# Last four gates and six query blocks as five Strassen pairs ahead of the state-space scan

## The chip, the cores and the metric

The kernel runs on one core of one Trainium2 chip. The metric is the device time of one execution in microseconds. PE is TensorE (its weight loads are shown as PEld), DVE is VectorE, ACT is ScalarE, POOL is GpSimd and SP is SyncE, which here mostly issues DMAs. "Us" counts from the start of the profiled span.

## The reference

One layer of a decoder for a prompt of 1024 tokens and a sample group of 8 tokens, 1032 columns in all, model width 1024, all in float32:

```python
sc_b, sc_c, sc_x, z, xbc, dt_raw, q, gates = jnp.split(xn @ w_in, splits, axis=-1)
y_a = (sc_b * conv_u) @ w_sc_out                       # gated convolution
y_ssd, ssm_new = ssd_fn(xs, dt, a, bm, cm, ssm_s0)     # chunked scan, 32 heads in 4 groups, 8 chunks of 128
y_ssd = (y_ssd + ssm_d[:, None] * xs).reshape(...) * jax.nn.silu(z)
y_b = group_rmsnorm(y_ssd, ssm_norm_w, SSM_GROUPS) @ w_ssm_out
y_c = jnp.einsum('bhlm,bmhd->blhd', probs, mem_v).reshape(...) @ w_attn_o
g_a, g_b, g_c = jnp.split(jax.nn.sigmoid(gates), N_BRANCHES, axis=-1)
merged = g_a * y_a + g_b * y_b + g_c * y_c             # then w_merge_o, the SwiGLU block, the last norm
```

The change concerns the columns `q` (1024, eight blocks of 128) and `gates` (3072, 24 blocks of 128) of the first product, and how the scan `ssd_fn` shares the time with products.

## The kernel before, in words

Activations lie transposed: 128 features on the partitions, 1032 columns. Every product is made with three passes (high by high, low by high, high by low parts of a float32 split in two), so a weight block is first split by one ACT cast (L167) and one DVE subtraction (L168).

A **plain block** (`gemm`, L199, matmuls of L219) makes 128 output features: 8 slices of the contraction by 3 passes by 3 column pieces (256, 512, 264), which is 72 matmuls into one of two PSUM buffers (`pmm`, L64). A **Strassen pair** (`strassen`, L310, matmuls of L265) makes two such blocks at once with 7 half-size products instead of 8: 7 by 4 slices by 3 passes by 2 pieces (256, 260), 168 matmuls, and some more additions on DVE and ACT. Nearly all blocks of the first product run as pairs, the last one being `gate_pair(18)`, tile names G18. Its hook `plain` (L1371) turns the activations back into the plain form and loads the data of the scan's first group.

Then comes the **scan stage**. Its products are 12 plain `fillers` (L1387: the eight query blocks, tiles `ps_q`, weights wq0 to wq7, and the gate blocks 20 to 23, tiles `ps_g`) and after them the `outs`: the eight blocks of the convolution's output product (weights wo00 to wo07), eight and eight of the state-space output product's two halves (wo10 to wo17 and wo20 to wo27), and the eight of the attention output (wo30 to wo37). The scan itself is cut into small pieces in the queue `pend`, 158 in all. While a plain block is recorded, `tick` (L183) takes pieces out of that queue; `pace` (L1470) sets how many for each block: `len(pend) / (len(fillers) + KD)`, KD being 8, so 158 pieces over 20 blocks. The later attention stage does the same with its own pieces (L1697): all of them over the blocks of `outs` that are still left, less one.

A chunk of the scan has three pieces. `first` (L996): PE makes bp (a transpose and the C by B product) and xp (four transposes); DVE makes cbm (L1008), multiplies it onto the decays r (L1011) and makes xdt (L1013); POOL makes xdd. `third` (L1049) of the chunk before: PE makes pss, DVE adds it to the state s (L1059). `second` (L1022): PE makes po from the state and py from r and xdt, DVE puts both into y (L1036, L1045). The decays are loaded (L979, 512 KB broadcast) and prepared on ACT (L985, L986).

Between two groups of heads lies a **turn**: `z_pieces` (L1126) and `group_norm` (L1146) on the finished group (DVE products and sums into sqa, then PE psny, a root on ACT, PE psnr, ACT copies, the DVE scaling L1177 and four stores to `yb_d`), and the load of the next group's data (L1364, L1368) into tiles that the finished group has held. The next group's chunk 0 needs them.

The inputs of the output products are read back from DRAM tile by tile ahead of time: `out_ahead` (L1411) loads two tiles, and hangs a function on the next block that splits tile k-2 and loads tile k while slice k is recorded (L1416). These tiles, called in00 to in07, like most evictions, come from the pool `ev` of five buffers (L60), which also holds the sums sqa and the final state sf of each group. The tiles b00 to b07 are their split forms and the moving operands of the blocks. The two halves of the state-space product read `yb_d`, which groups 1 and 2 and then groups 3 and 4 of the scan have written.

All of this is recorded as one program, and a scheduler then places the instructions engine by engine: what is recorded first goes first if it can, otherwise later work goes ahead. The resulting order on each engine and in each DMA queue is fixed in the built program.

## Time and profile before

| | |
|---|---|
| Time, median of 3 runs | 2478.05 us (2475.4 to 2478.8) |
| The profiled execution | 2481.63 us, its span 2479.3 us |
| PE busy in the span | 98% |
| DVE, ACT, POOL busy | 64%, 43%, 5% |
| DMA, mean over the span | 163 GB/s |
| G18, the last pair, starts | 940.0 us |
| wq0, first plain block of the scan stage, starts | 960.8 us |
| wo10, first block of the state-space output, starts | 1317.4 us |
| wo30, first block of the attention output, starts | 1586.3 us |

PE is busy nearly everywhere, so the program is read as PE's own work plus the short times in which PE waits. A row of the timeline gives start, duration, engine, line, operation, out<-in by the program's names, and in brackets how long the engine was idle before it and for whom.

### The profile page before, as it was taken

What the parts mean: (1) busy time and instruction counts of PE and PEld (TensorE: products, weight loads), DVE (VectorE), ACT (ScalarE), POOL (GpSimd) and SP (SyncE); (2) the same over time, 40 slices, a digit from 0 to 9 for tenths busy, and PEclk for the clock granted to TensorE, in tenths of its full rate; (3) what the DMA queues carried; (4) which work ended last, traced back from release to release, by engine and by line L of the source; (5) the groups of instructions that cost most, each with busy time, mean ns of one, the idle gap of its engine ahead of it and who ended that gap; (6) DMA issues with size and microseconds to landing.
All of it is one profiled execution on the core that took longest, in us unless ns stands there. A gap on an engine that the chain in (4) does not pass through costs nothing.

```text
span 2479.3 us, 45686 instructions
## 1 busy us (share of the span) xinstructions
PE 2433.7 (98%) x18946; PEld 2312.4 (93%) x18946; DVE 1586.1 (64%) x2601; ACT 1067.9 (43%) x1714; POOL 114.3 (5%) x163
## 2 busy tenths in 40 slices
PE   8999999999999999999999999999999999999998
PEld 6899999999999999888888887899999999999998
DVE  6744586777677774667767562454787555476755
ACT  6554455453555535556445441223443333342322
POOL 0100000000000000121120000000000000000000
PEclk9999999999999999999999999999999999999999
DMA  6344435344344456668878687774453323264421
GB/s 197 112 145 154 129 103 154 111 128 117 123 132 142 128 154 209 194 207 267 264 217 275 204 272 238 258 239 154 143 174 129 112 82 112 77 234 127 154 85 69
DMA packets 359662, 404.42 MB, mean 163 GB/s; under 512 B 17446, under 2 KB 286870, under 8 KB 359447
## 3 DMA queue, kind: packets, MB, share of 16 engines
q1 hardware_dynamic: 339006, 343.79, 44.5%
q10 hardware_dynamic: 20449, 57.71, 6.0%
q8 instruction: 149, 2.44, 0.4%
q14 instruction: 58, 0.48, 0.1%
HBM read 286.35 MB, written 115.32 MB: 162 GB/s over the span
## 4 chain that ended last, share of the span: by engine, by line
PE 84%; DMA 6%; DVE 6%; ACT 2%; issue 1%; SPq 0%; ACTq 0%; DVEq 0%; POOL 0%
PE po L219 12%; PE ps_q L219 4%; PE pm L1799 4%; PE ps_g L219 2%; PE pd L219 1%; PE py L1040 1%; PE pss L1053 1%; PE po L1032 1%; PE Z2m L265 1%; PE d02m L265 1%; PE ps_z L219 1%; PE Z4m L265 1%; PE X8m L265 1%; PE C1m L265 1%; PE G18m L265 1%
## 5 line engine op out<-in xcount | busy, mean ns | idle before, releaser
L985 ACT ACTIVATE r<-r,acum 128x128 f32<-128x128 f32 x256 | 79.3, 392 | 4.3 <-DMA r<-ac_d 3.9
L756 DVE SCALAR_TENSOR_TENSOR ax<-u,prm,ax 128x1024 f32<-128x1024 f32 x44 | 56.4, 1281 | 0.0
L926 ACT ACTIVATE st<-st,es 128x128 f32<-128x128 f32 x128 | 41.5, 392 | 28.6 <-DMA st<-in_state_ssm_dram 23.0
L1017 POOL TENSOR_TENSOR xdd<-xdt,decst 128x512 f32<-128x512 f32 x32 | 38.9, 1215 | 287.7 <-DVE xdt L1013 287.7
L1446 DVE TENSOR_TENSOR yr<-po,yr 128x1032 f32<-128x1032 f32 x8 | 9.8, 1230 | 55.9 <-PE po L219 45.0
L1036 DVE TENSOR_TENSOR y<-po,ea 128x512 f32<-128x512 f32 x28 | 19.3, 690 | 37.5 <-PE po L1032 37.3
L1011 DVE TENSOR_TENSOR r<-r,cbm 128x1024 f32<-128x1024 f32 x32 | 39.2, 1224 | 2.4
L928 DVE SCALAR_TENSOR_TENSOR st<-sr,dts,st 128x128 f32<-128x128 f32 x128 | 40.2, 345 | 0.4
L1010 ACT COPY bT<-bp 128x128 f32<-128x128 f32 x32 | 8.5, 265 | 69.8 <-DVE cbm L1008 69.7
L2033 ACT ACTIVATE fj<-psy 128x512 f32<-128x512 f32 (+1 forms) x18 | 10.7, 595 | 59.1 <-PE psy L2031 59.0
L932 DVE SCALAR_TENSOR_TENSOR sr<-st,sr 128x128 f32<-128x128 f32 x128 | 35.3, 285 | 1.1
L1040 PE MATMUL py<-r,xdt 128*64 128x128 f32 x512 | 35.0, 279 | 0.0
L986 ACT ACTIVATE r<-r 128x1024 f32<-128x1024 f32 x32 | 33.9, 1058 | 0.6
L1053 PE MATMUL pss<-xdd,bT 128*128 128x512 f32 x64 | 33.4, 604 | 0.5 <-ACT bT L1010 0.5
L1806 DVE TENSOR_TENSOR x<-pm,xT 128x516 f32<-128x516 f32 x16 | 11.1, 695 | 35.1 <-PE pm L1799 35.1
L1013 DVE TENSOR_TENSOR xdt<-xp,dtT 128x512 f32<-128x512 f32 x32 | 21.9, 685 | 17.8 <-PE xp L1006 17.6
L1040 PEld LDWEIGHTS py<-r,xdt 128*64 128x64 f32 x512 | 27.3, 136 | 4.2 <-issue 0.5
L1032 PE MATMUL po<-bc,s 128*128 128x128 f32 x224 | 29.8, 276 | 1.0 <-DVE s L1059 1.0
L1066 POOL TENSOR_TENSOR s<-s,cdec 128x512 f32<-128x512 f32 x28 | 30.2, 1078 | 7.6 <-DVE s L1059 7.2
L1032 PEld LDWEIGHTS po<-bc,s 128*128 128x128 f32 x224 | 27.6, 191 | 2.8 <-issue 1.6
L1728 DVE TENSOR_TENSOR gt<-po,gt 128x1032 f32<-128x1032 f32 x8 | 9.8, 1231 | 30.1 <-PE po L219 27.1
L759 DVE SCALAR_TENSOR_TENSOR ax<-u,prm,ax 128x1032 f32<-128x1032 f32 x22 | 28.3, 1288 | 0.0
(9066 smaller groups left out, 8985.7 us busy)
## 6 DMA issues: line engine op xcount, KB each, us to landing
r<-ac_d SPq DMA_DIRECT2D x32, 512.0 KB
gt<-gt_d SPq DMA_DIRECT2D x24, 516.0 KB
xs_d<-ax ACTq DMA_DIRECT2D x22, 516.0 KB
gt_d<-G ACTq DMA_DIRECT2D x20, 516.0 KB
x<-xs_d SPq DMA_DIRECT2D x16, 516.0 KB
zs<-zs_d SPq DMA_DIRECT2D x16, 516.0 KB
yb_d<-x SPq DMA_DIRECT2D x16, 516.0 KB
in<-yb_d SPq DMA_DIRECT2D x16, 516.0 KB
```

Source lines behind the costliest of these rows:

```text
L219: PE.matmul(out[:, c : c + n], wt[:, ks], x[:, c : c + n], start=(k == 0 and i == 0), stop=(k == nk - 1 and i == 2),)
L265: PE.matmul(hv(ps)[:, c : c + n], wt[:, ks], x[:, c : c + n], start=(start and kt == 0 and i == 0), stop=(kt == 3 and i == 2), skip_group_ ...
L756: V.scalar_tensor_tensor(acc[:, :T], u[:, j : j + T], w[j], acc[:, :T], op0=ALU.mult, op1=ALU.add)
L926: S.activation(st[:, i], st[:, i], AF.Copy, scale=es[:, g * 4 + i, b : b + 1])
L928: V.scalar_tensor_tensor(st[:, i], rb, dts[:, g * 4 + i, b : b + 1], st[:, i], op0=ALU.mult, op1=ALU.add)
L985: S.activation(r[:, j, :], r[:, j, :], AF.Relu, scale=-1.0, bias=acum[:, c, h : h + 1])
L1011: V.tensor_tensor(r, r, bc(cbm.unsqueeze(1), [P, HPG, P]), op=ALU.mult)
L1017: G.tensor_tensor(b3(xdd, HPG), b3(xdt, HPG), bc(decst[:, c, hs].unsqueeze(2), [P, HPG, 64]), op=ALU.mult)
L1032: PE.matmul(po[:, t * P : (t + 1) * P], state["s"][:, t * P : (t + 1) * P], bcg[1][:, cs], start=True, stop=True,)
L1040: PE.matmul(py[hp : hp + 64, (h // 2) * P : (h // 2 + 1) * P], xdt[:, h * 64 : (h + 1) * 64], r[:, (h % 2) * 4 + h // 2, :], start=True, s ...
L1053: PE.matmul(pss, bT, xdd, start=True, stop=True)
L1799: PE.matmul(hv(ps)[:, c : c + n], wt[:, ks], x[:, half * HT + c : half * HT + c + n], start=(k == 0 and i == 0), stop=(k == KD - 1 and i = ...
```

## The change

Query blocks 0 to 5 and gates 20 to 23 leave the fillers and become five Strassen pairs (`q_pair`, new, and the known `gate_pair`) right after `gate_pair(16)` and ahead of `gate_pair(18)`. Two fillers stay, wq6 and wq7. The pieces of the scan are now spread over 2 + 8 + 3 = 13 blocks, three of them from the state-space output product, and the attention stage, which starts with what is left of `outs`, has its pieces spread over three blocks fewer.

```diff
--- before.py
+++ after.py
@@ -808,15 +808,6 @@
 
         return [Step(wblock(w_in, C_Q + i * P), f"wq{i}", s)]
 
-    def gate_step(i):
-        def s():
-            ps = proj(C_G + i * P, f"g{i}")
-            t = ev_tile(f"g{i}")
-            S.activation(t[:, :TT], flat(ps), AF.Sigmoid)
-            S.dma_start(gt_d[i], t[:, :TT])
-
-        return [Step(wblock(w_in, C_G + i * P), f"wg{i}", s)]
-
     def xbc_conv(ct, u, name):
         G.memset(u[:, 0:3], 0.0)
         G.tensor_copy(tail_xc[:, ct // 8, :, ct % 8], u[:, T : T + 11])
@@ -877,6 +868,21 @@
 
     def z_pair(i, hook=None):
         plain_pair(C_Z, zs_d, i, "Z", AF.Silu, hook)
+
+    def q_pair(i):
+        os = []
+
+        def outs():
+            os.extend([pa_["u"](f"Q{i}"), pa_["u"](f"Q{i + 1}")])
+            return os[0][:, HS[0]], os[0][:, HS[1]], None, os[1][:, HS[1]]
+
+        pa = strassen(
+            wblock(w_in, C_Q + i * P), wblock(w_in, C_Q + (i + 1) * P), xforms, f"Q{i}", pa_["s"], outs
+        )
+        S.activation(os[1][:, HS[0]], pa, AF.Copy, scale=-1.0)
+        for j, t in enumerate(os):
+            G.tensor_copy(qs[:, i + j, :], t[:, T:TT])
+            S.dma_start(q_d[i + j], t[:, :TT])
 
     def gate_pair(i, after_t3=None):
         plain_pair(C_G, gt_d, i, "G", AF.Sigmoid, None, after_t3)
@@ -1351,6 +1357,10 @@
     with_steps(3, lambda: z_pair(14))
     with_steps(2, lambda: gate_pair(16))
     assert not steps
+    for i in range(0, 6, 2):
+        q_pair(i)
+    for i in (20, 22):
+        gate_pair(i)
     rb = ev_tile("rb")
     SY.dma_start(rb[:, :TT], r_d.to_broadcast([P, TT]))
     b12s = []
@@ -1369,7 +1379,7 @@
             xg.append(t)
 
     def plain():
-        loaded["wq0"] = load_raw(wblock(w_in, C_Q), "wq0")
+        loaded["wq6"] = load_raw(wblock(w_in, C_Q + 6 * P), "wq6")
         load_group(0)
         for kt in range(4):
             split_to(*xforms["T3"][kt], b12s[kt // 2][:, HS[kt % 2]])
@@ -1385,10 +1395,8 @@
     for name in ("ssr", "ssd", "ssy"):
         pool[name] = ssd.enter_context(tc.tile_pool(name=name, bufs=2, side="right"))
     fillers = deque()
-    for i in range(8):
+    for i in range(6, 8):
         fillers.extend(q_step(i))
-    for i in range(20, 24):
-        fillers.extend(gate_step(i))
 
     acts = []
 
@@ -1467,7 +1475,7 @@
         pend.append(lambda g=g, hold=hold: [z_load(g, t, hold) for t in range(2)])
         pend.extend(pieces[-3:])
         pend.extend(z_pieces(g, xg, hold) + [None] + group_norm(g, xg, hold))
-    pace[:] = len(pend) / (len(fillers) + KD) + 1e-6, 0.0
+    pace[:] = len(pend) / (len(fillers) + KD + 3) + 1e-6, 0.0
     while fillers or pend:
         if len(fillers) == 1:
             out_ahead(sc_d)
```

What the scheduler makes of it, in numbers of plain matmuls that stand on PE between one py and the next (72 are one block):

| PE, scan stage | before | after |
|---|---|---|
| bp of group 1 chunk 0 to its py | 72 | 52 |
| group 2, chunks 1 to 7 | 11 13 13 22 27 27 36 | 12 13 19 13 13 13 13 |
| group 3, chunks 1 to 7 | 18 24 27 30 18 19 21 | 11 12 6 19 11 0 0 |
| turn from group 1 to 2, py to py | 202 | 214 |
| turn from group 2 to 3 | 203 | 191 |
| turn from group 3 to 4 | 220 | 71 |

The first place is PE at the end of group 3's scan (names with 2_6 and 2_7 are its chunks 6 and 7; po01 and po10 are plain blocks). Before:

```order
L1002 MATMUL bp2_7_13514<-ident_75,bc162_12830 128x128
L1003 MATMUL bp2_7_13514<-bc202_12832,bc162_12830 128x128
L219 MATMUL po01_13461<-b02h_13094,wo01l_13458 128x256
L219 MATMUL po01_13461<-b02h_13094,wo01l_13458 128x512
L219 MATMUL po01_13461<-b02h_13094,wo01l_13458 128x264
L219 MATMUL po01_13461<-b03h_13123,wo01h_13457 128x256
L1006 MATMUL xp2_7_13517<-ident_75,x20_12834 128x128
L1006 MATMUL xp2_7_13517<-ident_75,x21_12836 128x128
L1006 MATMUL xp2_7_13517<-ident_75,x22_12838 128x128
L1006 MATMUL xp2_7_13517<-ident_75,x23_12840 128x128
L219 MATMUL po01_13461<-b03h_13123,wo01h_13457 128x512
L1053 MATMUL pss2_6_13540<-xdd2_6_13441,bT2_6_13436 128x512
```

After:

```order
L1008 MATMUL bp2_7_14171<-ident_75,bc162_13627 128x128
L1009 MATMUL bp2_7_14171<-bc202_13629,bc162_13627 128x128
L1012 MATMUL xp2_7_14174<-ident_75,x20_13631 128x128
L1012 MATMUL xp2_7_14174<-ident_75,x21_13633 128x128
L1012 MATMUL xp2_7_14174<-ident_75,x22_13635 128x128
L1012 MATMUL xp2_7_14174<-ident_75,x23_13637 128x128
L1059 MATMUL pss2_6_14197<-xdd2_6_14118,bT2_6_14113 128x512
L1038 MATMUL po2_7_14215<-bc202_13629,s2_6_14132 128x128 x4
L1046 MATMUL py2_7_14221<-r2_7_14049,xdt2_7_14184 64x128 x8
L1059 MATMUL pss2_7_14240<-xdd2_7_14186,bT2_7_14181 128x512
L1081 MATMUL psf2_14266<-ident_75,s2_7_14200 128x128 x4
L219 MATMUL po10_14471<-b02h_14344,wo10h_14467 128x256
```

Before, plain matmuls of wo01 stand between the scan's. After, nothing stands between them from chunk 6 on, and the first plain matmul behind the last chunk needs b02, the split of in02.

The second place is the DMA queue of SP where the inputs of wo10 are loaded from `yb_d` (in00 to in07; r and ea are the scan's decays, 2_7 being group 3's last chunk and 3_0 to 3_2 group 4's first). Before:

```order
L1399 DMA in00_14540<-yb_d_122 128x1032
L1440 DMA mg_d_125<-gt06_14376 128x1032
L1399 DMA in01_14542<-yb_d_122 128x1032
L1533 DMA kc00_14862<-in_cache_mem_k_dram 128x1024
L1399 DMA in02_14582<-yb_d_122 128x1032
L1399 DMA in03_14601<-yb_d_122 128x1032
L1399 DMA in04_14616<-yb_d_122 128x1032
L1533 DMA kc01_14914<-in_cache_mem_k_dram 128x1024
L139 DMA wo14r_15231<-in_w_ssm_out_dram 128x8x128
L1440 DMA mg_d_125<-gt07_14538 128x1032
L1399 DMA in05_14648<-yb_d_122 128x1032
L1399 DMA in06_14663<-yb_d_122 128x1032
```

After, where in00 and in01 stand some twenty rows further up:

```order
L985 DMA r3_2_14502<-ac_d_138 128x1024
L999 DMA ea3_1_14543<-ea_d_139 64x512
L1407 DMA in02_14310<-yb_d_122 128x1032
L1084 DMA out_p_ssm_dram<-sf2_14271 128x4x128
L1407 DMA in03_14333<-yb_d_122 128x1032
L1407 DMA in04_14348<-yb_d_122 128x1032
L1374 DMA bc163_14420<-xs_d_128 128x1032
L1378 DMA x30_14424<-xs_d_128 128x1032
L1378 DMA x32_14428<-xs_d_128 128x1032
L1407 DMA in05_14380<-yb_d_122 128x1032
```

Before, the whole scan is over when these inputs are loaded. After, in02 stands behind decay loads of group 4 (chunks 1 and 2), which go into buffers that group 3's last chunks hold, and in03 and in04 behind the store of group 3's final state.

The third place is PE at the end of the attention stage, where psob transposes the sample's attention rows (they are then stored to `at_d`, from which wo30 reads). Before:

```order
L219 MATMUL po27_17129<-b01h_16033,wo27h_17125 128x256
L219 MATMUL po27_17129<-b01h_16033,wo27h_17125 128x512
L219 MATMUL po27_17129<-b01h_16033,wo27h_17125 128x264
L1607 MATMUL psob_17080<-ident_75,osr_17078 128x8 x8
L219 MATMUL po27_17129<-b01l_16034,wo27h_17125 128x256
L219 MATMUL po27_17129<-b01l_16034,wo27h_17125 128x512
L219 MATMUL po27_17129<-b01l_16034,wo27h_17125 128x264
```

After:

```order
L219 MATMUL po27_17353<-b05l_16225,wo27h_17349 128x256
L219 MATMUL po27_17353<-b05l_16225,wo27h_17349 128x512
L1615 MATMUL psob_17304<-ident_75,osr_17302 128x8 x8
L219 MATMUL po27_17353<-b05l_16225,wo27h_17349 128x264
L219 MATMUL po27_17353<-b05h_16224,wo27l_17350 128x256
L219 MATMUL po27_17353<-b05h_16224,wo27l_17350 128x512
```

Before, psob stands 12 matmuls into wo27, with 60 left; after, 50 matmuls into it, with 22 left.

## Prediction

> **What bounds the kernel now.** I read the page first, then the busy times of chosen stretches, then what PE waited for. The page's head and its first section:
>
> ```profile
> span 2479.3 us, 45686 instructions
> PE 2433.7 (98%) x18946; PEld 2312.4 (93%) x18946; DVE 1586.1 (64%) x2601; ACT 1067.9 (43%) x1714; POOL 114.3 (5%) x163
> ```
>
> PE is the bound over the whole program. So there are two sums: what PE no longer has to do, and how long it newly stands still. The stretches (from:to, length, busy time of PE, PEld, DVE, ACT and POOL with instructions, PE clock, DMA):
>
> ```profile
> 900.00:960.00 60.00, 60.00 (x507) 60.00 (x506) 32.96 (x53) 27.04 (x35) 0.00 (x0) 1.00 0.58 185
> 960.00:1317.00 357.00, 355.48 (x2561) 306.54 (x2560) 239.19 (x296) 199.54 (x413) 70.67 (x68) 1.00 0.73 231
> 1317.00:1586.00 269.00, 257.92 (x1703) 222.38 (x1702) 132.61 (x315) 95.23 (x187) 0.00 (x0) 0.99 0.74 246
> 1586.10:1589.50 3.40, 3.21 (x10) 2.51 (x11) 3.27 (x3) 2.20 (x3) 0.00 (x0) 0.50 0.39 112
> 1622.20:1667.40 45.20, 45.20 (x289) 40.99 (x288) 22.30 (x19) 6.37 (x7) 0.00 (x0) 1.00 0.70 228
> ```
>
> The first row holds three pairs of 168 matmuls: 20.0 us a pair. The last holds four plain blocks of 72: 11.3 us a block, 0.157 us a matmul. The second is the scan stage: 20 blocks are 226 us of its 357, the other 131 are the scan's own PE work, and PE stands still for 1.5 us. In the attention stage, third row, it stands still for 11. The fourth row is for the clock, below.
>
> That the scan costs PE no waiting today does not mean that it is fast. Its own rhythm is seen where it has run closest together, in group 2. All DVE instructions of one chunk there:
>
> ```profile
> 1074.75 0.69 DVE L1045 TENSOR_TENSOR y<-py,y 128x512 f32<-128x512 f32 x1 [0.34 <-PE py L1040]
> 1075.36 0.28 DVE L1008 TENSOR_TENSOR cbm<-bp,tri 128x128 f32<-128x128 f32 x1
> 1075.74 1.23 DVE L1011 TENSOR_TENSOR r<-r,cbm 128x1024 f32<-128x1024 f32 x1
> 1076.88 0.68 DVE L1013 TENSOR_TENSOR xdt<-xp,dtT 128x512 f32<-128x512 f32 x1
> 1077.49 0.68 DVE L1059 TENSOR_TENSOR s<-pss,s 128x512 f32<-128x512 f32 x1
> 1079.52 0.69 DVE L1036 TENSOR_TENSOR y<-po,ea 128x512 f32<-128x512 f32 x1 [1.36 <-PE po L1032]
> ```
>
> The next y<-py starts 1.04 us after the last row (0.69 of work, 0.34 of waiting for py, as in the first row), at 1080.56: a circle of 5.8 us. PE's po waits for s, DVE's y for po, the next cbm for y. Nothing in the circle is spare, so 5.8 us is what a chunk takes by itself. The order has 13 plain matmuls in that chunk (2.0 us), so PE's own part of a chunk is 3.8 us.
>
> The turn between two groups is slower. Chosen rows of the turn from group 1 to 2, py to py:
>
> ```profile
> 1029.76 1.09 PE L1040 MATMUL py<-r,xdt 128*64 128x128 f32 x16
> ...
> 1046.70 2.07 PE L1153 MATMUL psny<-ones,sqa 128*128 128x1 f32 x18
> ...
> 1053.98 4.91 DVE L1177 SCALAR_TENSOR_TENSOR x<-x,prm,sqa 128x1032 f32<-128x1032 f32 x4 [3.13 <-ACT sqa L1173]
> 1055.30 3.94 SPq L1180 DMA_DIRECT2D yb_d<-x  x4
> ...
> 1059.33 1.46 SPq L1368 DMA_DIRECT2D x<-xs_d  x2
> ...
> 1067.91 1.09 PE L1040 MATMUL py<-r,xdt 128*64 128x128 f32 x16
> ```
>
> The finished group is normed (17 us to psny, 7 more to the scaling, 5 of scaling), stored, and only then come the last two loads of the next group's x, into the tiles that the stores free: 38.2 us. PE does 202 plain matmuls in it, 31.7 us, and 6.5 us of the scan's.
>
> **The change part by part.**
>
> *Ten blocks become five pairs.* 10 x 11.3 = 113.0 us of PE work becomes 5 x 20.0 = 100.0: -13.0 us, and this is all that the change can gain. The pairs' additions, casts and stores cost nothing, since DVE and ACT are busy for 33 and 27 us of 60 in the first row above and DMA for 0.58 of the time; without that cover a pair would take its DVE time, 11 us, which is below 20. Their ten weight loads stand on SP's queue and their ten stores on ACT's ahead of those of G18, where before they stood among the scan's loads; nobody waits there. The scan's own instructions stay the same in number.
>
> *The start of the scan.* Before, 72 plain matmuls stand between xp and py of the first chunk, after, 52, which is 8.2 us:
>
> ```profile
> 960.84 0.74 PE L219 MATMUL ps_q<-xnh,wq0h 128*128 128x256 f32 x3
> ...
> 970.20 0.18 DVE L1083 COPY y<-ys 128x32 f32<-128x32 f32 x1 [8.55 <-DMA gt_d<-G]
> 970.30 1.22 DVE L1011 TENSOR_TENSOR r<-r,cbm 128x1024 f32<-128x1024 f32 x1
> ```
>
> DVE is stopped there until the gate tile of G18 is stored, and that is in the change as well: py can start at 971.6 at the earliest, PE would be there at 969.0. +2.6 us (0 if the store lands early, 4 if late).
>
> *Chunks of group 3.* 13 plain matmuls fill a chunk's 5.8 us. After, chunks 3 to 7 have 6, 19, 11, 0 and 0. Chunk 3 has three splits more on DVE (wo12, b00, b01; a split of a block is 1.22 us in the turn's stretch), one of them between s and po, so I give it 7.0 us: 3.8 + 0.9 of work, 2.3 us of waiting. Chunk 4 none, chunk 5 0.3, chunks 6 and 7 2.0 each. Together 6.6; I take +6 (3 if po and py answer faster in an empty queue, 9 if the splits cost in full).
>
> *The turn from group 3 to 4.* The cover of the turn is gone. The two blocks wo10 and wo11 hold both PSUM buffers, and beyond their first two slices they need in02 to in07, whose loads stand behind group 4's decays and the final state on SP. These wait for py and psf of group 3's last chunk; behind them on the same queue wait in03 to in07 and the x tiles of group 4. In the order 71 plain matmuls are left in the turn, 11.1 us, with 6.5 of the scan's: 17.6 us of work. I take the turn at 37 us: the chain above less about 1 us in which psnr had only waited its place on PE. That is 19.4 us of waiting: +19.5. Bounds: 34 us (16.5) if the last x loads land sooner, 41 us (23.5) by the slowest turn:
>
> ```profile
> 1209.59 0.66 PE L1040 MATMUL py<-r,xdt 128*64 128x128 f32 x8
> ...
> 1250.67 0.44 PE L1040 MATMUL py<-r,xdt 128*64 128x128 f32 x4
> ```
>
> *The other turns* have 214 and 191 matmuls, 33.6 and 30.0 us, with 6.5: 40 and 36.5 against 37. +1 (0 to 4).
>
> *The attention stage* has the same pieces over 12 blocks, not 15. What PE waited for there:
>
> ```profile
> PE psp L1646 <- DVE pTl L1654: 3.0, 2, 2.2
> PE psa L1632 <- ACT pr L1552: 2.8, 2, 1.7
> PE po L219 <- ACT b00h L177: 2.2, 1, 2.2
> PE pskT L1519 <- DVE kTl L1522: 1.7, 1, 1.7
> ```
>
> Without the third row this is 7.5 us of waiting for DVE and ACT. A fifth less filler between the steps makes it half as much again at a guess: +3 (0 if the pieces still fit, 8 if it doubles). DVE is busy for half of this stage, so it does not become the bound.
>
> *The end of the attention stage.* The third row is the wait of wo30 for the sample rows, whose chain begins with psob:
>
> ```profile
> 1573.76 0.66 PE L1607 MATMUL psob<-ident,osr 8*128 8x8 f32 x8
> ...
> 1578.70 3.95 SPq L1399 DMA_DIRECT2D in<-at_d  x3
> ...
> 1586.25 0.58 PE L219 MATMUL po<-b00h,wo30h 128*128 128x256 f32 x1 [2.19 <-ACT b00h L177]
> ```
>
> 12.5 us from psob to wo30, in which 60 plain matmuls (9.4 us) and psob leave 2.2 to wait. After, 22 are left: 38 fewer are 6.0 us: +6 (4 to 7).
>
> *The clock.* Right behind that wait of 2.2 us lies the row 1586.1:1589.5 with a clock of 0.50. Half the clock for 3.4 us costs at most 1.7 us where PE is busy. The turn's waiting will come in some four pieces, but PE's work there is late anyway, so only psny, psnr and xp on the chain count: +2 (0 to 6).
>
> The Trainium skill, TensorE: Matmul & The Clock Gate, Part 1, says that the clock is halved after at least one idle window of about 3.4 us. The trace halves it after 2.2 us of idleness, so here the measurement decides. By the page the short waits would keep the full clock and the sum would be 1 to 2 us lower.
>
> The sum: -13.0 + 2.6 + 6 + 19.5 + 1 + 3 + 6 + 2 = +27.1 us. The profiled execution took 2481.63 us, so 2508.7; the median is 3.6 us lower, 2478.05, and against it I forecast 2505.2.
>
> **The rivals.**
>
> *The scan answers faster than its rows (not slower).* PE was never idle in this stage, so 5.8 and 38 us may be times in PE's queue more than the scan's own. If an empty queue brought the turn down to 20 us, the waits of the turn, chunks, start and end would shrink to some 2.4, 1, 0 and 3, with 2 for attention: -13 + 8.4 = -4.6, 2473.5. It decides from a turn of about 24 us down. Against it: DVE alone is busy for most of the first 17 us and for the 5 of scaling, and the loads follow the stores.
>
> *Only the turn is shorter*, 31 us, and the clock and attention cost nothing: -13 + 2.6 + 6 + 13.5 + 6 = +15, 2493. The x loads take up to 7 us each with DMA at 0.73 of its time; with PE and its evictions still, they may take less.
>
> *The attention stage starves too.* Its steps wait on DVE, which has 133 us to do in what would be 13 x 11.3 + 77 = 224 us (257.9 less 16 blocks is 77), and the loads of the same bytes are pressed together. If its 11 us of waiting become 25, that is 11 more than my 3: +38, 2516.
>
> *The change does not do what it says*, the pairs stalling without side work: the pairs of the first row run at 20.0 us with little beside them, so this is worth 1 or 2 us at most.
>
> **How the numbers follow.** A measurement of this kernel tells 0.2%, 5 us, from no change. Forecast (2498 to 2512): 0.6. Only the turn shorter (2483 to 2498): 0.13. Attention starved (2512 to 2525): 0.17. Within 5 us: 0.05. Faster: 0.05. The range of 8 in 10 reaches from 2490 to 2519: 0.14 is left out below (faster, within 5 us and a third of the shorter turn) and 0.06 above (a third of the starved attention). Faster 0.05, same 0.05, slower 0.90.
>
> **What would show it.** Right: five pairs of 20 us each behind G16; in group 3's last two chunks a py every 5.8 us with no ps or po of a plain block between them; then a turn of some 37 us in which PE is busy for half, its waits put down to b02 to b06 and to sqa; psob less than 4 us ahead of wo27's end and 8 us of waiting for b00 behind it; clock marks of 0.50 in the turn. Wrong: a turn below 25 us, or PE idle for less than 13 us more than before. If PE waits for as long as I say, but in the attention heads, the mechanism is wrong and the size an accident.

## The result, and the profile after

| | before | after |
|---|---|---|
| Median | 2478.43 us (2475.40 to 2481.28, 4 runs) | 2518.47 us (2511.70 to 2523.83, 4 runs) |
| Profiled execution, its span | 2481.63, 2479.3 us | 2518.46, 2516.7 us |

After to before is 1.0161, 95% interval 1.0149 to 1.0173: slower by 40 us. The forecast was 2505.2 (2490 to 2519), 27.1 us slower.

The page of the kernel after, its head and first section:

```profile
span 2516.7 us, 46021 instructions
PE 2438.1 (97%) x19066; PEld 2323.1 (92%) x19066; DVE 1617.3 (64%) x2646; ACT 1074.9 (43%) x1732; POOL 117.5 (5%) x163
```

PE has 120 matmuls more (840 for five pairs less 720 for ten blocks), which should be 13 us less of work. It is busy for 4.4 us *more*. It stands still for 78.6 us instead of 45.6. Both have to be explained. Plain matmuls below are those of plain blocks (L219). Stretches of the kernel after (from:to, length, busy time of PE, PEld, DVE, ACT, POOL, then PE clock and DMA), in this order: six pairs (the five new ones and G18), the scan to the last psnr of group 4, in it the turns from group 2 to 3 and from group 3 to 4, then the attention stage to psob, and psob to wo30:

```profile
937.00:1057.00 120.00, 120.00 (x1010) 120.00 (x1010) 55.68 (x70) 42.98 (x59) 3.95 (x6) 1.00 0.43 138
1057.75:1401.10 343.35, 312.30 (x2168) 261.51 (x2167) 240.64 (x302) 187.75 (x403) 69.53 (x62) 0.94 0.73 233
1203.80:1247.90 44.10, 41.89 (x250) 36.93 (x249) 29.55 (x33) 14.26 (x23) 0.08 (x1) 0.88 0.78 257
...
1293.40:1332.20 38.80, 25.52 (x130) 20.79 (x129) 28.61 (x32) 17.15 (x26) 0.45 (x1) 0.69 0.72 253
1401.10:1615.10 214.00, 203.34 (x1340) 174.50 (x1338) 114.92 (x295) 78.34 (x169) 0.00 (x0) 0.98 0.76 255
1615.10:1625.80 10.70, 4.27 (x31) 3.66 (x30) 4.43 (x6) 1.66 (x2) 0.00 (x0) 0.85 0.90 292
```

The same two stages before (the scan to psnr of group 4, and attention to psob):

```profile
960.84:1327.90 367.06, 365.54 (x2628) 315.72 (x2627) 246.35 (x305) 204.60 (x419) 70.67 (x68) 1.00 0.74 233
1327.90:1573.80 245.90, 236.76 (x1559) 203.44 (x1559) 121.97 (x301) 87.66 (x178) 0.00 (x0) 0.99 0.72 241
```

The scan stage holds 1487 plain matmuls before and 1025 after, counted in the traces between the starts of the py groups; at 0.157 us that is 72.5 us less. The stage became only 23.7 us shorter. The other 48.8 us are the cost: PE stands still for 31.1 us in it instead of 1.5, which is 29.5, and the other 19.3 are slower work. What each part takes beyond its plain matmuls (length less 0.157 each):

| us beyond plain work | before | after | more | forecast |
|---|---|---|---|---|
| start to the first py | 0.2 | 1.4 | 1.2 | 2.6 |
| group 1, chunks 1 to 7 | 26.3 | 31.7 | 5.4 | 0 |
| turn 1 to 2 | 6.4 | 6.7 | 0.3 | together 1 |
| group 2 | 26.5 | 26.8 | 0.3 | 0 |
| turn 2 to 3 | 6.6 | 14.1 | 7.5 | (above) |
| group 3 | 28.7 | 36.2 | 7.5 | 6 |
| turn 3 to 4 | 6.5 | 27.6 | 21.1 | 19.5 |
| group 4 | 26.7 | 29.3 | 2.6 | 0 |
| last turn, to psnr | 5.6 | 8.5 | 2.9 | 0 |
| attention to psob | 81.8 | 84.5 | 2.7 | 3 |
| psob to wo30 | 3.1 | 7.3 | 4.2 | 6 |

The sum is 55.7 us. Take off 13.0 for the pairs and 5.2 by which the parts ahead of the pairs (3.1) and behind wo30 (2.1) were shorter in this execution, and 37.5 are left; the spans differ by 37.4. In the runs below (e5 and e6 apart, which change the outer parts) these stand between +2.8 and -6.7 us from the same execution of before, at -3.1 in one without any pair (e7), so I take the 5.2 for no part of the change.

What PE waited for between 1057 and 1626 us after (in total, times, longest):

```profile
PE po L219 <- ACT b00h L177: 6.4, 1, 6.4
PE pss L1059 <- ACT bT L1016: 5.0, 4, 2.3
PE po L219 <- DVE b02l L178: 4.5, 1, 4.5
PE po L219 <- ACT b02h L177: 4.4, 1, 4.4
PE po L1038 <- DVE s L1065: 4.0, 4, 1.6
...
PE bp L1008 <- DVE y L1042: 3.2, 3, 1.4
...
PE po L219 <- DVE gt L1447: 2.2, 1, 2.2
PE po L219 <- DVE b05l L178: 2.0, 1, 2.0
```

Of the rows shown, 1, 3, 4 and 8 are splits of new inputs, 5 and 6 the scan's own circle, as forecast. Rows 2 and 7 were not forecast. The longest wait of row 2 in the timeline, in group 1:

```profile
1092.18 1.38 SPq L1407 DMA_DIRECT2D in<-sc_d  x3
...
1093.91 1.05 ACT L177 CAST b03h<-in 128x1032 fp32r<-128x1032 f32 x1 [3.88 <-DMA in<-sc_d]
...
1094.87 0.26 ACT L1016 COPY bT<-bp 128x128 f32<-128x128 f32 x1
...
1095.28 1.10 PE L1059 MATMUL pss<-xdd,bT 128*128 128x512 f32 x2 [2.29 <-ACT bT L1016]
```

bp is made by 1091.0, but its copy bT stands behind the cast b03h on ACT, and that one waits for a load. Row 7, in the turn from group 2 to 3:

```profile
1217.42 1.22 DVE L1146 TENSOR_TENSOR sqa<-sqa,zs 128x1032 f32<-128x1032 f32 x1
...
1218.57 1.22 DVE L1447 TENSOR_TENSOR gt<-po,gt 128x1032 f32<-128x1032 f32 x1
...
1219.85 1.23 PE L219 MATMUL po<-b00h,wo06h 128*128 128x256 f32 x3 [2.19 <-DVE gt L1447]
...
1222.37 3.83 PE L1159 MATMUL psny<-ones,sqa 128*128 128x1 f32 x18
```

wo06 needs a PSUM buffer that DVE empties only behind the turn's sums. Then psny takes 3.83 us, where it took 2.07 before: the clock. The turn from group 3 to 4, the largest term:

```profile
1293.38 1.09 PE L1046 MATMUL py<-r,xdt 128*64 128x128 f32 x16
...
1301.12 1.05 ACT L177 CAST b02h<-in 128x1032 fp32r<-128x1032 f32 x1 [1.68 <-DMA in<-yb_d]
...
1302.22 1.23 PE L219 MATMUL po<-b02h,wo10h 128*128 128x256 f32 x3 [4.37 <-ACT b02h L177]
...
1307.54 1.22 DVE L178 TENSOR_TENSOR b02l<-in,b02h 128x1032 fp32r<-128x1032 f32 x1
...
1308.81 1.23 PE L219 MATMUL po<-b02l,wo10h 128*128 128x256 f32 x3 [4.50 <-DVE b02l L178]
...
1310.05 3.91 PE L1159 MATMUL psny<-ones,sqa 128*128 128x1 f32 x18
...
1320.54 4.90 DVE L1183 SCALAR_TENSOR_TENSOR x<-x,prm,sqa 128x1032 f32<-128x1032 f32 x4 [3.95 <-ACT sqa L1179]
...
1321.86 3.93 SPq L1186 DMA_DIRECT2D yb_d<-x  x4
...
1332.16 1.98 PE L1046 MATMUL py<-r,xdt 128*64 128x128 f32 x16
```

It is 38.8 us from py to py, with the chain that the prediction gave, and PE stands before b02 twice. The first time the cast b02h waits for the load of in02; the second time b02l stands on DVE behind the turn's products and sums. The clock behind the wait for wo06 and behind the first wait for b02:

```profile
1219.70:1229.90 10.20, 10.05 (x40) 9.38 (x41) 3.35 (x9) 1.04 (x2) 0.00 (x0) 0.50 0.88 308
1298.20:1318.70 20.50, 11.97 (x45) 10.60 (x46) 14.97 (x19) 8.82 (x10) 0.00 (x0) 0.50 0.76 272
```

### The profile page after: what moved, and what is told of

It is laid out like the page before. It is cut to its first block, busy times and chain, and to the rows that moved or that the text cites. A ratio compares the mean times of both kernels' runs of the same rounds, so it can differ in the third digit from the quotient of the medians.

```text
span 2516.7 us, 46021 instructions
## 1 busy us (share of the span) xinstructions
PE 2438.1 (97%) x19066; PEld 2323.1 (92%) x19066; DVE 1617.3 (64%) x2646; ACT 1074.9 (43%) x1732; POOL 117.5 (5%) x163
## 4 chain that ended last, share of the span: by engine, by line
PE 84%; DMA 6%; DVE 6%; ACT 2%; issue 1%; SPq 0%; ACTq 0%; DVEq 0%; POOL 0%
PE po L219 11%; PE pm L1807 3%; PE pd L219 1%; PE pss L1059 1%; PE py L1046 1%; DMA ea<-ea_d 1%; PE Z4m L265 1%; PE ps_z L219 1%; PE C6m L265 1%; PE X8m L265 1%; PE Z2m L265 1%; PE d16m L265 1%; PE C7m L265 1%; PE Q4m L265 1%; PE Z14m L265 1%
## 5 line engine op out<-in xcount | busy, mean ns | idle before, releaser
L932 ACT ACTIVATE st<-st,es 128x128 f32<-128x128 f32 x128 | 41.5, 392 | 26.5 <-DMA st<-in_state_ssm_dram 23.7
L1454 DVE TENSOR_TENSOR yr<-po,yr 128x1032 f32<-128x1032 f32 x8 | 9.9, 1232 | 51.9 <-PE po L219 39.4
L1042 DVE TENSOR_TENSOR y<-po,ea 128x512 f32<-128x512 f32 x28 | 19.3, 690 | 31.7 <-PE po L1038 23.3
L2041 ACT ACTIVATE fj<-psy 128x512 f32<-128x512 f32 (+1 forms) x18 | 10.7, 596 | 59.3 <-PE psy L2039 59.2
L992 ACT ACTIVATE r<-r 128x1024 f32<-128x1024 f32 x32 | 33.8, 1058 | 0.6
L1183 DVE SCALAR_TENSOR_TENSOR x<-x,prm,sqa 128x1032 f32<-128x1032 f32 x16 | 19.6, 1288 | 16.5 <-ACT sqa L1179 16.5
L1019 DVE TENSOR_TENSOR xdt<-xp,dtT 128x512 f32<-128x512 f32 x32 | 21.9, 684 | 11.5 <-PE xp L1012 11.3
```

The lines of the kernel that those rows point to most:

```text
L932: S.activation(st[:, i], st[:, i], AF.Copy, scale=es[:, g * 4 + i, b : b + 1])
```

## The experiments

The first theory: the loss sits where a change of inputs (wo00 or wo10, whose tiles must be loaded and split) meets a turn. Its rival: too few plain blocks beside the scan, wherever they lie.

**e1, only the pieces spread over 13 blocks**, on the kernel before:

```diff
-    pace[:] = len(pend) / (len(fillers) + KD) + 1e-6, 0.0
+    pace[:] = len(pend) / (len(fillers) + 1) + 1e-6, 0.0
```

> The kernel before, without any new pair; only the scan's 158 pieces are spread over 13 blocks instead of 20 (12 of the plain query and gate blocks and wo00). First theory (the loss sits where a change of inputs meets a turn: the next product's tiles come through the five buffers of ev and through SP behind the scan, so nothing plain can be placed there): the order has 209 and 199 plain matmuls in the first two turns but 76 in the turn from group 3 to 4, although enough blocks are left and their inputs have lain in DRAM for long. So the first two turns stay at 38 us, the third takes 37 to 39 us with some 19 us of waiting, nothing else loses over 2 us: 2495 to 2501 us. Rival (the tiles of wo10 are late because group 2 of the scan has only just written them): wo00's are not written by the scan, so no wait, 2478 us. Second rival (13 blocks are too few for the scan everywhere): the waits spread over all groups and turns, about the 46 us that the changed kernel lost in the scan, 2524 us.

2507.33 us, ratio 1.0124 (1.0109 to 1.0139). The first two turns lost 1.2 and 1.9 us, the third 15.3, although wo00's inputs are old. PE waits there for sqa (second row), and right behind the scan's last psnr once more for a PSUM buffer (first row), as wo06 above:

```profile
PE po L219 <- DVE gt L1439: 13.0, 1, 13.0
PE psny L1153 <- DVE sqa L1140: 11.2, 1, 11.2
```

The wait of 13.0 us already belongs to the attention stage. So the lateness of group 2's output isn't needed for the loss. The largest loss is where the first theory put it; but the start (3.0), groups 1 and 4 (2.6 and 2.8) and attention (4.1) lost too, and the time is 6 us over its range.

**e2, six of the last blocks**, on the kernel after: `KD + 3` becomes `KD + 6`.

> The changed kernel with its five pairs, the scan spread over 16 blocks instead of 13 (six of the state-space output instead of three). First theory: the turns now have 209, 207 and 169 plain matmuls, so the third turn waits for 4 us instead of 21 of own time too much, chunks of group 3 none; what is left is -13 for the pairs, 4 for the splits in group 1, 4 for the turn, 12 for the end of attention (3 plain matmuls stand between psob and wo30) and 6 for a thinner attention stage: +13 against the kernel before, 2491 us. Rival (it is the number of blocks that the scan shares, wherever they lie): 4 of the 7 blocks are still missing, 4/7 of 46 us, and the attention stage loses double: +28, 2506 us.

2505.18 us, ratio 1.0113 (1.0099 to 1.0127). The third turn lost 6.0 us instead of 21.1 and the whole scan stage 12.8 instead of 48.8: this part was right. The attention stage, three blocks poorer, lost 19.3 and its end 7.7 (PE waits 10.1 us for b00 there, against 6.4): 27.0 together, where 6 and 12 were expected. The blocks were only lent. The time is the rival's, but not at the rival's places.

**e3, four pairs**, on the kernel after: gates 22 and 23 are plain fillers again, `KD + 4`.

```diff
-    for i in (20, 22):
+    for i in (20,):
         gate_pair(i)
...
+    for i in (22, 23):
+        fillers.extend(gate_step(i))
```

> The changed kernel with four pairs instead of five (gates 22 and 23 stay plain blocks of the scan) and the scan over 16 blocks, four of them of the state-space output. First theory: the turns have 259, 196 and 214 plain matmuls and no chunk has fewer than 11, so the scan loses no more than 4 us (start and splits of group 1); -10.4 for the pairs, 8 to 9 at the end of attention (11 plain matmuls left), 4 for attention, 2 for the clock: +5 to +8 against the kernel before, 2484 to 2487 us. Rival (number of blocks): -10.4 + 26 + 13 - 5 = +24, 2502 us.

2511.04 us, ratio 1.0132 (1.0115 to 1.0149): the scan stage lost 31.7 us, attention and its end 13.4. The time is above both, and nearer to the rival. But the scan's loss lies in three turns: 5.9 us in the one from group 1 to 2, where wo00 begins, 10.7 in the one from 3 to 4, where PE waits for b02 of wo10, and 11.9 in the last, which has 51 plain matmuls and where PE waits 7.8 us for sqa at a stretch. So the first theory's limit of 4 us for 259, 196 and 214 plain matmuls does not hold.

```profile
PE psny L1168 <- DVE sqa L1155: 8.4, 2, 7.8
...
PE po L219 <- ACT b02h L177: 5.1, 1, 5.1
```

**e4, two pairs**: only the gates move, all eight query blocks stay fillers, `KD + 0`.

```diff
-    for i in range(0, 6, 2):
-        q_pair(i)
...
-    for i in range(6, 8):
+    for i in range(0, 8):
         fillers.extend(q_step(i))
```

> The changed kernel with two pairs instead of five (gates 20 to 23; all eight query blocks stay plain blocks of the scan), the scan over 16 blocks, none of the state-space output. First theory: the turns have 205, 243 and 208 plain matmuls and no chunk has fewer than 11, the end of attention keeps its 66: -5.2 for the pairs, +1 at the start, +2 for splits in group 1: -2 against the kernel before, 2476 us (2473 to 2479). Rival (number of blocks): 4/7 of 46 us, -5.2 + 26 - 3 = +18, 2496 us.

2501.69 us, ratio 1.0096 (1.0082 to 1.0110), 26 over the first theory. Its places are right, though: 10.0 us in the turn from group 2 to 3, where wo00 begins, 16.2 in the last turn, which has 31 plain matmuls and in which wo10, begun shortly before it, waits for its split inputs, and 4 in all the rest of the scan. PE's waits, 6.3 us of the first in the last turn, the second in the turn from group 2 to 3:

```profile
PE po L219 <- DVE b02l L178: 6.8, 2, 6.3
...
PE po L219 <- DVE b03l L178: 3.0, 1, 3.0
```

The count of plain matmuls did not tell that the turn of 243 would take 54.7 us.

**e5 and e6, the clock by itself**, on the kernel before. POOL does nothing else in this stage; stops is ('T1', 'T3', 'T4') with one multiplication in e5, ('T1',) with three in e6, for 6 <= j < 20. `in_turn` ties the order of PE only; in these pairs it holds the products' matmuls as well.

```diff
             st_prod(forms, ps, w, off, f, start)
+            if f in stops:
+                p = sm_ps("stop")
+                t = stopt[0]
+                in_turn("pe", PE.transpose(p[:, :P], t[:, 0], ident))
+                G.tensor_tensor(t, t, ident.unsqueeze(1).to_broadcast([P, 3, P]), op=ALU.mult)
+                in_turn("pe", PE.transpose(p[:, P : 2 * P], t[:, 0], ident))
```

> The kernel before, with 42 short stops of PE in 14 pairs of the feed-forward stage (three in a pair, behind the products T1, T3 and T4): PE transposes a tile, POOL multiplies it once (128x384), PE transposes it again, and only then goes on. The tile is read by nobody else. A stop should be some 0.9 us of POOL and 0.5 us of handing over and transposing, 1.4 us, idle for 1.1 to 1.3. First theory (the clock is halved behind a wait that fills over half of a window of 3.4 us): these are too short, no marks of 0.50 in this stage, and the cost is the stops themselves, 42 x 1.4 = 59: 2536 us. Rival (any wait cools the clock in proportion): about half as much again, 2565 us.

> As the short stops, but 14 of them (one in a pair, behind T1) with POOL multiplying the tile three times: about 3.1 us each, idle for some 2.8. By themselves they cost 14 x 3.1 = 43 us, 2520 us, less than the 42 short ones. First theory (a wait of over 1.7 to 2 us in one window of 3.4 halves the clock for the next): at least two in three of the 14 are followed by marks of 0.50, each for 3.4 us or more, 1.7 us lost in each window: 16 to 24 us more, 2536 to 2544 us, and up to 2590 us if the half clock holds for three windows. Rival (only a window that is idle as a whole halves it): no marks, 2520 us.

2551.76 us, ratio 1.0292 (1.0274 to 1.0309), and 2555.84, ratio 1.0310 (1.0295 to 1.0326). The waits of e5, then its stretch from 1900 us:

```profile
PE stop L354 <- POOL stop L353: 53.6, 42, 2.6
```

```profile
1900.00:2200.00 300.00, 253.29 (x2061) 244.88 (x2060) 139.45 (x175) 77.29 (x101) 39.49 (x36) 0.99 0.24 79
```

And of e6:

```profile
PE stop L356 <- POOL stop L355: 52.4, 14, 4.8
```

```profile
1900.00:2200.00 300.00, 254.28 (x1952) 251.50 (x1952) 125.73 (x166) 75.78 (x100) 41.47 (x36) 0.91 0.23 76
```

The idle time is nearly the same in both, 53.6 and 52.4 us, and PE waits for nothing else in this stage; yet the clock falls only in e6. A short stop costs 72.2 / 42 = 1.72 us, 1.28 of it idle and 0.44 for transposing and handing over. 14 long ones would by that be 52.4 + 14 x 0.44 = 58.6 us; they cost 76.3. The 17.7 us over are put down to the half clock: 13 of the 14 are followed by marks of 0.50, 61 us of them in all, and in e5 only the first stop is, the one of 2.6 us. By its marks the first theory holds in both. Its times were 16 and 12 us too low (2536, and 2536 to 2544), since the stops themselves had been priced too low: 1.4 us for a short one and 43 us for the 14 long ones.

**e7, the scan two blocks later**, nothing else, on the kernel before:

```diff
-    pace[:] = len(pend) / (len(fillers) + KD) + 1e-6, 0.0
+    pend.extendleft([None] * 16)
+    pace[:] = len(pend) / (len(fillers) + KD + 2) + 1e-6, 0.0
```

> The kernel before with no pair moved and with its own pace of 7.9 pieces for each block; 16 empty pieces stand in front of the scan, so that it starts and ends two blocks later. As many plain blocks stand beside each group as before. First theory (what costs is a change of inputs that falls into a turn): wo00 now begins in the turn from group 2 to 3 (behind psf of group 2, as in the kernel with two pairs, which lost 10 us there), wo10 in a chunk of group 4, and 31 instead of 60 plain matmuls stand between psob and wo30: +6 to +10 in that turn, 0 to 2 at wo10, 2 to 4 at the end of attention, +10 to +14 against the kernel before, 2487 to 2491 us. Rival (what costs is too few blocks beside the scan): only the end of attention, +3, 2480 us.

2477.34 us, ratio 0.9994 (0.9985 to 1.0003). The first theory falls: wo00 begins in a turn, and that turn loses only 1.2 us. The whole scan stage lost 3.3 us and the end of attention 2.6; the attention stage took 6.8 less, for which no cause was found. The turn, py to py:

```profile
1204.80:1257.10 52.30, 50.10 (x365) 42.51 (x365) 40.30 (x49) 27.64 (x60) 11.22 (x10) 1.00 0.78 234
```

It is nearly as long as in e4, with DVE busy for 40 us, but 284 plain matmuls lie in it, and PE waits for 2.2 us. In these runs a change of inputs in a turn did harm only where the plain work was short as well.

**e8, the turn's tiles in buffers of their own**, on the kernel after, against the prediction's "loads stand behind" on SP:

```diff
-            sf = ev_tile(f"sf{g}", (P, 4, P))
+            sf = b3(sp_tile([P, 512], "xdt", f"sf{g}"), 4)
...
-                hold["q"] = ev_tile(f"sqa{g}")
+                hold["q"] = hold["y"][:, 0, :]
...
-            t = hold["r"] = ev_tile(f"nr{g}")
+            t = hold["r"] = sp_tile([P, 27], "nr", f"nr{g}", 1)
```

> The changed kernel with its five pairs and its pace; the sum of squares sqa lies in the first quarter of the group's y (which its first piece has used up), the final state in a buffer of xdt and the roots in a small tile of their own, so that nothing of a turn takes one of the five buffers of ev. The loads in02 to in06 now stand on SP ahead of group 3's last two chunks. The order has 25, 13, 13, 12 and 0 plain matmuls in chunks 3 to 7 of group 3 (6, 19, 11, 0, 0 in the changed kernel) and 40 in the turn from group 3 to 4 (71). If the five buffers and the queue of SP made the loss of that turn, as the prediction put it: the turn loses no more than 5 us, 2500 us. If the splits of wo10's inputs are held as well by the other ring (the twelve act tiles, shared with zs and x) and by DVE's work in the turn: group 3 loses 1 to 2 us instead of 7.5, the turn 25 instead of 21, 2515 to 2518 us.

2517.08 us, ratio 1.0154 (1.0139 to 1.0170): as the kernel after. in02 to in06 are loaded early now, and the wait has moved on to later tiles (waits first, then two rows of the turn):

```profile
PE po L219 <- DVE b05l L178: 6.2, 1, 6.2
...
PE po L219 <- ACT b07h L177: 3.4, 1, 3.4
```

```profile
1304.88 1.04 ACT L177 CAST b05h<-in 128x1032 fp32r<-128x1032 f32 x1
...
1313.02 1.23 DVE L178 TENSOR_TENSOR b05l<-in,b05h 128x1032 fp32r<-128x1032 f32 x1
```

b05h is cast by 1305.9, but DVE makes b05l only at 1313.0, behind the turn's products and sums. Group 3 lost 4.1 us instead of 7.5, the turn 22.5 instead of 21.1, near the second expectation (1 to 2, and 25), whose time was met. The whole scan stage lost 39.4 instead of 48.8, but attention 13.7 instead of 2.7, most of it in one wait of 10.1 us for a load (kk from `k_d`). So the queue of SP is not needed for the turn's loss.

**e9, one pair, and e10, two pairs with 18 blocks.** On the kernel before: `gate_pair(22)`, or `gate_pair(20)` and `gate_pair(22)`, ahead of `gate_pair(18)`, their plain steps taken out, and

```diff
-    pace[:] = len(pend) / (len(fillers) + KD) + 1e-6, 0.0
+    pace[:] = len(pend) / (len(fillers) + KD + 2) + 1e-6, 0.0
...
-        pace[:] = len(pend) / (len(outs) - 1) + 1e-6, 0.0
+        pace[:] = len(pend) / (len(outs) - 2) + 1e-6, 0.0
```

> One pair only (gates 22 and 23) ahead of the scan, and the scan still over 20 blocks (ten plain ones and ten of outs); the attention stage's pieces end one block earlier (len(outs) - 2). The order is that of the kernel with the later scan: turns of 202, 292 and 209 plain matmuls, no chunk under 11, wo00's change inside the turn of 292, and 94 instead of 60 plain matmuls between psob and wo30. Theory as it stands now (a wait comes where the plain matmuls in a turn run out: about 200 for a turn, some 290 for one in which the tiles of new inputs are split as well, 111 for the last): nothing runs out, so -2.6 for the pair, -2 to -3 at the end of attention, 0 to +1 elsewhere: -3 to -5, 2474 to 2477 us. Rival (any plain block taken out of the scan's time costs something, 46 us for seven): two blocks fewer in all cost some 5 to 13, 2480 to 2490 us.

> Two pairs (gates 20 to 23), the scan over 18 blocks instead of the 16 of the earlier kernel with two pairs, and the attention stage's pieces one block earlier. The turns have 203, 245 and 205 plain matmuls, the last one 116 (31 in the earlier kernel), no chunk under 11. Theory as it stands now: the loss of 16 in the last turn goes; the turn of 245, in which wo00's change falls, still lacks some 40 matmuls, 6 us, and 2 to 3 for the clock; -5.2 for the pairs, -2 at the end of attention: 0 to +4 against the kernel before, 2479 to 2483 us. Rival (only the sum of plain matmuls beside the scan counts, 1370 here, and 1312 would fill it): -5 to -7, 2473 us. Rival (number of blocks): 2500 us.

e9: 2471.20 us, ratio 0.9977 (0.9968 to 0.9986), 6 us below the kernel before and 3 below the range expected. e10: 2473.21, ratio 0.9986 (0.9976 to 0.9995). Their scan stages, e9's first:

```profile
979.70:1348.60 368.90, 364.04 (x2607) 313.95 (x2606) 248.71 (x308) 203.34 (x418) 67.89 (x68) 1.00 0.72 235
```

```profile
997.60:1355.20 357.60, 350.46 (x2512) 299.75 (x2512) 247.06 (x306) 197.22 (x412) 73.85 (x68) 1.00 0.74 238
```

PE waits for 4.9 and 7.1 us, the clock is at 1.00. The scan stages still lost 5.2 and 8.9 us; the attention stage took 7.0 and 2.8 less, its end 2.4 less in both. e10's turn of 245 plain matmuls lost 0.6 us, so "some 290 for a turn with a change" was wrong; the rival by the sum, 2473, was right there.

**e11, attention earlier**, on the kernel after: `len(outs) - 1` becomes `len(outs) - 3`.

> The changed kernel with its five pairs, and only the attention stage's pieces spread over two blocks fewer (len(outs) - 3): 145 instead of 22 plain matmuls between psob and wo30, the same before that stage. If the 4 us at the end of attention come from the missing cover behind psob: they go, with half a clock window, and the thinner stage before it gives 0 to 3 back: -2 to -6, 2513 to 2517 us. If wo30 waits for something else (its weights, or the loads of at_d): no change, 2518.5 us.

2521.24 us, ratio 1.0181 (1.0167 to 1.0195), above both forecasts. The end lost nothing any more (0.7 us beyond plain work instead of 7.3), but the stage before it went from 84.5 to 95.3. Its largest wait:

```profile
PE pso L1607 <- DMA vc<-in_cache_mem_v_dram: 4.7, 1, 4.7
```

**e12, e9 without its pair**: e7 with `len(outs) - 2`.

> The kernel before with no pair moved, with the two small changes of place that the one-pair kernel has: the scan two blocks later (16 empty pieces in front, the same pace) and the attention stage's pieces one block earlier. Its order is that of the one-pair kernel but for two plain blocks more in front of the scan. If the gain of the one-pair kernel (6 us) comes mostly from where the work lies: 2473 to 2475 us, 3 to 5 below the kernel before, and the pair itself is worth the 2.6 us that two plain blocks and a pair differ by. If the pair makes it all: 2477 us.

2476.56 us, ratio 0.9996 (0.9985 to 1.0007): the shifts alone bring nothing that can be measured. e9 stands 0.0019 lower, about 5 us give or take 3.5, and 2.6 lies within that.

The scan stages side by side (first plain block to the last psnr; "beyond" is length less 0.157 for each plain matmul, and includes 132 us of the scan's own work; in e7 and e12 two of the blocks lie ahead of the scan's first piece):

| kernel | plain matmuls | blocks of 72 | length, us | beyond |
|---|---|---|---|---|
| e12 | 1610 | 22.4 | 390.7 | 137.9 |
| e7 | 1610 | 22.4 | 389.7 | 136.9 |
| before | 1487 | 20.7 | 367.1 | 133.6 |
| e9 | 1466 | 20.4 | 368.9 | 138.8 |
| e10 | 1370 | 19.0 | 357.6 | 142.5 |
| e2 | 1241 | 17.2 | 341.3 | 146.4 |
| e3 | 1236 | 17.2 | 359.4 | 165.3 |
| e4 | 1216 | 16.9 | 354.7 | 163.8 |
| e1 | 1080 | 15.0 | 329.8 | 160.2 |
| e8 | 1075 | 14.9 | 341.7 | 173.0 |
| after | 1025 | 14.2 | 343.4 | 182.4 |
| e11 | 1025 | 14.2 | 340.4 | 179.5 |

This is the theory that is left: the scan has a length of its own, and taking plain work away from beside it does not make the stage shorter than that. In the four kernels with 14 to 15 blocks, and in e2 with 17.2, the stage took 330 to 343 us. No run goes below 14.2 blocks, so the floor is inferred, not shown. From 20.7 to 19.0 blocks (e10) 9.5 of the 18.4 us that were taken out came off the stage, down to 17.2 (e2) 25.8 of 38.6; from there to 14.2 (after, e11) nothing more, though e1, with 15.0 blocks lying otherwise, was 11.5 us shorter than e2. The change took out 6.4 blocks, 72.5 us, for 23.7. Where the blocks run out decides over some 17 to 19 us more: e2, e3 and e4 hold nearly the same number. In e4 the two turns in which new inputs are waited for lose; in e3 two such turns and the last. No run took these turns of e3 apart, so their causes stay open.

## Why the prediction was right and where it failed

- **Pairs at 20.0 us, -13.0**: right. 120.00 us for six, PE busy throughout.
- **The sign and the mechanism**: right. PE stands still for 33.0 us more in the whole program, in the turn above all. The time, 2518.5, lies inside the range by 0.5 us, while the four executions lie between 2511.7 and 2523.8; that it is inside is luck. The parts of the table cost 55.7 us where the terms of the forecast, clock included, came to 40.1, and the outer parts, which the change does not touch, were 5.2 us shorter in this execution.
- **The turn from group 3 to 4, +19.5**: right in size (21.1) and length (38.8 us for 37). The link that it named, the queue of SP behind the scan, shows in the first of the two waits for b02 only, and failed in e8: with the loads ahead of it the tiles wait for DVE, which is busy with the turn's own sums. Of the turn's 38.8 us PE is busy for 25.5, not for half, where 17.6 would do at full clock. The prediction argued that half clock costs little there since the chain sets the end; no run measured it apart, and psny, which is on the chain, took 3.91 us for 2.07.
- **Group 3, +6**: 7.5 by the circle of s, po and y. Py came after 7.1 and 6.9 us in chunks 6 and 7, not after 5.8; in chunk 7 bT stood behind decays on ACT:

```profile
1287.90 2.15 ACT L991 ACTIVATE r<-r,acum 128x128 f32<-128x128 f32 x7 [1.32 <-DMA r<-ac_d]
...
1289.96 0.24 ACT L1016 COPY bT<-bp 128x128 f32<-128x128 f32 x1
...
1290.35 1.10 PE L1059 MATMUL pss<-xdd,bT 128*128 128x512 f32 x2 [1.28 <-ACT bT L1016]
```

- **The start, +2.6**: 1.2, and by the profile DVE was held by ACT's decays and not by the gate tile, as the same DVE row after shows:

```profile
1065.93 0.18 DVE L1089 COPY y<-ys 128x32 f32<-128x32 f32 x1 [7.38 <-ACT r L992]
```

- **The other turns, +1**: failed, 7.8. The step compared 191 plain matmuls with a turn of 37 us and found 36.5 us of work. It did not ask whether PSUM would be free for them: wo06 had to wait 2.2 us behind DVE's sums, and half clock followed.
- **The clock, +2**: failed. PE's work in the scan stage should take 1025 x 0.157 + 132.1 (before: 365.5 busy less 1487 x 0.157) = 293.0 us and took 312.3. Of the 19.3 us over, 16.4 lie in the four parts whose clock was below 1.00: 7.8 in the turn from group 3 to 4, 5.3 in the one from 2 to 3, where a wait of 2.19 us was followed by 10.2 us at 0.50, and 3.3 in group 4 and the last turn (0.96 and 0.93). The step took 3.4 us of half clock behind a wait, counted only the chain's own matmuls in it, and gave nothing to the other turns. The Trainium skill, TensorE: Matmul & The Clock Gate, Part 1, says that the window of 3413 ns runs free; the marks of each run agree, they lie on one grid of 3.41 us. The Trainium skill, TensorE: Matmul & The Clock Gate, Part 1, also says that the clock is halved after at least one idle window. If that means a window idle as a whole, e6 contradicts it: there 1.92 us of idle time in a window were enough.
- **Costs put at nothing**: group 1 lost 5.4 us, 3.7 of them in waits for bT. With two fillers instead of twelve the splits of wo00's inputs come into group 1, ahead of bT on ACT. The prediction gave no term to moved splits there. Group 4 and the last turn lost 2.6 and 2.9: 1.0 and 1.2 in waits for DVE (y and sqa), the rest in work at half clock.
- **Attention +3, its end +6**: 2.7 and 4.2 (a wait of 6.4 us for b00, not 8). As two separate terms they are misleading: e11 removed the second and got 10.8 us in the first.
- **The rivals**: a faster scan and a shorter turn are out (38.8 us; 33.8 in e1, the shortest). "Attention starves, 2516" gave nearly the measured time by the wrong stage: attention and its end lost 6.9 us, the scan 48.8.

## What to carry to other kernels

A chain that runs beside filler has a length of its own; first work out that length (here 28 chunks at 5.8 us, three turns at 38, a start of 10 and an end of 24 make 310; 330 to 343 were measured with 14 to 17 blocks) and move filler away only as far as the stage stays longer. Here, beyond that, a block was paid for where it went and saved nothing where it had been. Price a wait of PE together with the half clock behind it, and ask of each plain block that is to cover a stall whether its tiles *and* its PSUM buffer come from an engine that the stall keeps busy.

## What the runs showed of the hardware that was not expected

The stretches at half clock (marks of 0.50) begin and end on a fixed grid of 3.41 us in each trace. Lay PE's matmuls over that grid at the stops of e5 and e6: windows of the grid in which PE was idle for up to 1.81 us were followed by full clock, windows with 1.92 us or more by half. So it is the idle time in one window that counts, not the length of the wait: a wait of 3.34 us that a border cut into 1.81 and 1.52 left the clock alone (the one of the 14).

Small matmuls count nearly as idleness. In e5 the window from 1132.5 us has no idle time by the trace, and half clock follows it all the same; 18 psny matmuls of one column fill the last 2 us of it:

```profile
1133.83 2.15 PE L1162 MATMUL psny<-ones,sqa 128*128 128x1 f32 x18
```

The same is seen in e4, e6, e10 and e12. Count as idle, then, also the time in which PE ran only matmuls of at most 16 columns. In all fourteen traces, from 60 us on, a window at full clock was followed by half whenever over 1.94 us of it was idle in that sense and never when less than 1.50 was; between the two both occur. A window that was itself at half clock was followed by full only when at most 0.67 us of it was idle, and by half only when at least 0.65 was. So in these traces the clock falls at about half a window of idleness, but comes back only behind a window that is some four fifths busy. The lengths fit: in e6 the half clock stayed for 3.4 us behind eight stops and for 6.8 behind the five whose next window was idle for 1.0 us or more; in the turn from group 2 to 3 it stayed for 10.2 us, since psny, itself slowed to 3.83 us, lies in the windows behind the wait.
